# Up-projections of two FFNs as seven block products, with hidden tiles through DRAM and stacked low-rank products

## The chip, the cores and the metric

The kernel runs on one core of a Trainium2 chip. The core has TensorE (PE in the profile, with its weight loads as PEld), VectorE (DVE), ScalarE (ACT), GpSimd (POOL) and SyncE (SP, which here issues most DMAs). The metric is the device time of one execution in microseconds; the number given for a kernel is the median of its runs.

## The reference

Two transformer blocks follow each other on 1024 tokens of 1024 features, in float32. In short:

```
# block 1
h = x + concat(pool_mixer, ssm_mixer) @ w_out
u = rmsnorm(h, norm_ffn)
h = h + (silu(u @ w_gate) * (u @ w_up)) @ w_down          # D_FF = 2816
x = rmsnorm(h, norm_final)
# block 2
z = rmsnorm(x, g_mix) @ w_in      # latents of MLA, r, k, v and low-rank inputs of RWKV, gates
w = w0 + tanh(w_lo) @ w2;  a = sigmoid(a0 + a_lo @ a2);  g = sigmoid(g_lo) @ g2   # ranks 64, 64, 128
x = x + (gate_a * mla(z) + gate_b * rwkv7(z)) @ w_out
u = rmsnorm(x, g_ffn)
x = x + square(relu(u @ w_ffn_up)) @ w_ffn_down           # D_FF_2 = 4096
x = rmsnorm(x + sigmoid(rmsnorm(x, g_ple) @ w_ple_gate) * (p @ w_ple_proj), g_final)
```

## The kernel before

Each float32 operand of a product is split into a high part (rounded to the matmul's type, a cast on ScalarE, L103 or L122) and a low part (the rest, a subtraction on VectorE, L104 or L124); `mm3` (L137) makes hi·hi, hi·lo and lo·hi, three matmuls of a 128x128 weight block with 512 columns each, accumulated in PSUM. `weights` (L127) loads 128x1024 raw weights into one of two buffers "wr" and splits them, into two buffers each of "wh" and "wl", or, kept longer, into slots "wk". `slot` hands out 128x1024 tiles of a common pool.

A *unit* (`unit_t`) is one tile of 128 outputs for all 1024 tokens: 2 halves of the tokens x 8 blocks of the input x 3 = 48 matmuls into a PSUM tile "big" of 128x1024, of which there are four (two in the RWKV stage). `norm_units` makes the first two units: transposes of the scaled tokens for one half, split into "hn" (L195 on ScalarE, L197 on VectorE), then the units' matmuls on it, then the other half.

`ffn` walks over the hidden tiles, 22 in FFN1 (gate and up for each) and 32 in FFN2, in chunks of three. Each hidden tile is activated (L667 and L668, or L674 and L675) and split, its w_down rows are loaded and split, and `tok_matmul` (L242) multiplies the chunk by w_down for 8 token tiles x 2 halves, which VectorE adds to the residual `res` in SBUF (L659).

`rwkv_z` (L924) makes the token-shifted r, k and v by units (`project`), and in `low_rank(0)` and `(1)` products with w2 and a2, on operands of 64 rows, 2 x 4 output tiles x 2 halves x 3 = 48 matmuls; each output goes through one of two buffers "zo" to DRAM (zr).

The program is written in this order, and a scheduler orders each engine's queue by priority of program order and by when it reckons things to be ready; the engines then run their queues in order, with semaphores between them.

## Time and profile before

| | |
|---|---|
| median of 3 runs | 2983.57 us (2983.23 to 2987.06) |
| profiled execution | 2986.8 us, span 2985.0 us, mean granted TensorE clock 0.98 |
| TensorE | busy 2885.8 us, 14937 matmuls recorded |
| VectorE, ScalarE, GpSimd | 1301.5, 842.9 and 159.6 us |
| DMA | 227.46 MB |

A busy engine at 97% with a chain that lies mostly on it says which engine sets the time; where it waits is seen from windows of the stages and from the timeline.

### The profile page before, as it was taken

Reading aid. Unit: us, or ns where it says so; the run is one execution under the profiler, and the core shown is the slowest. Engines: PE = TensorE matmul, PEld = TensorE weight load, DVE = VectorE, ACT = ScalarE, POOL = GpSimd, SP = SyncE. Lnnn points to the kernel's source line nnn. Section 1 sums busy time; section 2 is a strip of 40 time slices with the busy share of each in tenths; the row PEclk is TensorE's granted clock in tenths of the full one; section 3 lists DMA queues with packets and bytes.
Section 4 is the critical chain, followed back from the end, with each engine's and each line's share of the span. In section 5 each row is a group of like instructions: output and inputs, shape, how many; then the busy total and the mean of one; then the engine's idle time right before and its main releaser. Section 6 shows DMA issues by size and latency. Waiting matters only on the chain.

```text
span 2985.0 us, 36005 instructions
## 1 busy us (share of the span) xinstructions
PE 2885.8 (97%) x14937; PEld 2299.3 (77%) x14937; DVE 1301.5 (44%) x1980; ACT 842.9 (28%) x1275; POOL 159.6 (5%) x343
## 2 busy tenths in 40 slices
...
GB/s 135 103 120 161 36 36 50 64 39 33 57 64 33 74 155 127 116 132 75 108 60 117 117 53 24 40 119 162 43 36 43 56 50 51 56 43 43 43 78 99
DMA packets 136115, 227.46 MB, mean 76 GB/s; under 512 B 60880, under 2 KB 82000, under 8 KB 135952
## 3 DMA queue, kind: packets, MB, share of 16 engines
...
## 4 chain that ended last, share of the span: by engine, by line
PE 85%; DVE 5%; POOL 3%; DMA 3%; ACT 2%; issue 2%; SPq 0%; ACTq 0%; DVEq 0%; POOLq 0%
PE big L139 25%; PE big L140 24%; PE big L141 24%; PE big L833 2%; POOL wt L1165 1%; POOL tt L1166 1%; PE ps L861 1%; PE ps L1137 1%; PE chain L855 1%; PE chain L854 1%; DVE t L836 0%; PE chain L139 0%; PE chain L140 0%; PE chain L141 0%; PE big L192 0%
## 5 line engine op out<-in xcount | busy, mean ns | idle before, releaser
L139 PE MATMUL big<-hn,wh 128*128 128x512 f32 x1872 | 747.2, 400 | 7.2 <-DVE zo L937 4.0
L140 PE MATMUL big<-hn,wh 128*128 128x512 f32 x1872 | 746.4, 399 | 1.9 <-DVE hn L197 1.9
L141 PE MATMUL big<-hn,wl 128*128 128x512 f32 x1872 | 744.0, 398 | 0.0
L139 PEld LDWEIGHTS big<-hn,wh 128*128 128x128 f32 x1872 | 353.2, 189 | 93.3 <-issue 5.9
L140 PEld LDWEIGHTS big<-hn,wh 128*128 128x128 f32 x1872 | 353.9, 189 | 86.5 <-DVE hn L197 3.2
L141 PEld LDWEIGHTS big<-hn,wl 128*128 128x128 f32 x1872 | 354.6, 189 | 85.0 <-DVE wl L104 2.5
L103 ACT CAST wh<-wr 128x1024 fp32r<-128x1024 f32 (+1 forms) x142 | 141.8, 999 | 935.0 <-PE big L140 742.0
L104 DVE TENSOR_TENSOR wl<-wr,wh 128x1024 fp32r<-128x1024 f32 (+1 forms) x142 | 166.1, 1170 | 425.7 <-ACT wh L103 424.9
L141 PE MATMUL big<-wk,a 128*128 128x512 f32 x864 | 338.4, 394 | 0.0
L140 PE MATMUL big<-wk,a 128*128 128x512 f32 x864 | 337.9, 393 | 0.1
L139 PE MATMUL big<-wk,a 128*128 128x512 f32 x864 | 334.7, 395 | 1.8 <-ACT wk L103 1.8
L659 DVE TENSOR_TENSOR r<-big,r 128x1024 f32<-128x1024 f32 x144 | 176.2, 1224 | 314.4 <-PE big L141 314.2
L139 PEld LDWEIGHTS big<-wk,a 128*128 128x128 f32 x864 | 160.9, 188 | 43.5 <-ACT wk L103 7.6
L140 PEld LDWEIGHTS big<-wk,a 128*128 128x128 f32 x864 | 162.2, 188 | 38.7 <-DVE wk L104 0.8
L141 PEld LDWEIGHTS big<-wk,a 128*128 128x128 f32 x864 | 162.2, 188 | 37.4
L674 ACT ACTIVATE zo<-big 128x1024 f32<-128x1024 f32 x32 | 32.9, 1027 | 368.3 <-PE big L141 368.3
L668 DVE TENSOR_TENSOR zo<-zo,big 128x1024 f32<-128x1024 f32 x22 | 26.9, 1221 | 205.7 <-PE big L141 205.7
L104 DVE TENSOR_TENSOR wk<-wr,wk 128x1024 fp32r<-128x1024 f32 (+1 forms) x86 | 100.3, 1173 | 31.6 <-ACT wk L103 31.5
L139 PE MATMUL big<-wk,mx 128*128 128x512 f32 x256 | 100.8, 400 | 2.6 <-ACT wk L103 2.6
L140 PE MATMUL big<-wk,mx 128*128 128x512 f32 x256 | 101.9, 398 | 1.0 <-DVE wk L104 1.0
L141 PE MATMUL big<-wk,mx 128*128 128x512 f32 x256 | 101.1, 395 | 0.0
L103 ACT CAST wk<-wr 128x1024 fp32r<-128x1024 f32 (+1 forms) x86 | 85.2, 1001 | 44.2 <-DMA wr<-in_w_out_dram 36.0
(408 smaller groups left out, 3639.4 us busy)
## 6 DMA issues: line engine op xcount, KB each, us to landing
wr<-in_w_ffn_up_dram SPq DMA_DIRECT2D x32, 512.0 KB, 3.2
wr<-in_w_ffn_down_dram SPq DMA_DIRECT2D x32, 512.0 KB, 3.2
zr<-zo SPq DMA_DIRECT2D x24, 512.0 KB, 3.5
wr<-in_w_gate_dram SPq DMA_DIRECT2D x22, 512.0 KB, 3.2
wr<-in_w_up_dram SPq DMA_DIRECT2D x22, 512.0 KB, 3.3
wr<-in_w_down_dram SPq DMA_DIRECT2D x22, 512.0 KB, 3.2
wr<-in_w_gates_dram SPq DMA_DIRECT2D x16, 512.0 KB, 4.6
gd<-zo SPq DMA_DIRECT2D x16, 512.0 KB, 3.1
```

Source lines behind the costliest of these rows:

```text
L103: nc.scalar.copy(hi, x)
L104: nc.vector.tensor_tensor(lo, x, hi.bitcast(F32), ALU.subtract)
L139: nc.tensor.matmul(ps, lhsT=w[0], rhs=x[0], start=start, stop=False)
L140: nc.tensor.matmul(ps, lhsT=w[0], rhs=x[1], start=False, stop=False)
L141: nc.tensor.matmul(ps, lhsT=w[1], rhs=x[0], start=False, stop=stop)
L659: nc.vector.tensor_tensor(res[t], ps, res[t], ALU.add)
L674: nc.scalar.activation(s, ps, AF.Relu)
L833: nc.tensor.matmul(sc[:, c:c + m], lhsT=q[:, i * P:(i + 1) * P], rhs=k[:, c:c + m], start=True, stop=c + m < n, skip_group_check=True)
L854: nc.tensor.matmul(acc[:, c0:H], lhsT=w, rhs=hi, start=t == 0, stop=False, skip_group_check=True)
L855: nc.tensor.matmul(acc[:, c0:H], lhsT=w, rhs=lo, start=False, stop=t == last, skip_group_check=True)
L861: nc.tensor.transpose(pt[:, j * P:(j + 1) * P], ps[j][:, t * P:(t + 1) * P], self.ident)
L1137: nc.tensor.matmul(ps[:, pt * P:(pt + 1) * P], lhsT=bk[c2][rows, c, pt, :, :], rhs=ar[c2][rows, c, pt, :, :], start=True, stop=True)
```

## The change

`ffn` stores `res` to DRAM (rd) at its start and reads it back before the down-projections. The input and two neighbouring hidden tiles are taken as 2 x 2 blocks, and a pair's up-projection is made with seven products of 4 input blocks x 3 = 12 matmuls instead of eight: `pair_weights` makes the sums S1 to S4 of weight blocks on GpSimd and splits them, `pair_products` accumulates the products in four PSUM tiles of 128x512 and puts the outputs together with copies on ScalarE and additions on VectorE and one on GpSimd. The sums T1 to T4 of input blocks are made by `sums` on GpSimd, while the first hidden tiles (two with gate and up in FFN1, four in FFN2) are made by units as before. `norm_blocks` makes plain float32 copies of the normed input ("bf") as well, for these sums, with the low part of the first four blocks on GpSimd. All hidden tiles are stored in DRAM (hd), read back and split in the down phase, whose chunks start with one tile (FFN1) or two (FFN2).

In `rwkv_z` the operands of low_rank(0) and (1) are stacked as high and low part in 128 rows, so two matmuls make what three made (32 in place of 48), and the outputs go to slot "z" instead of "zo", those of `project` too.

Lines taken out stand in the kernel above; of the diff's new lines these matter:

```diff
...
+    def mm3(self, ps, w, x, start, stop, **kw):
+        nc = self.nc
+        nc.tensor.matmul(ps, lhsT=w[0], rhs=x[0], start=start, stop=False, **kw)
+        nc.tensor.matmul(ps, lhsT=w[0], rhs=x[1], start=False, stop=False, **kw)
+        nc.tensor.matmul(ps, lhsT=w[1], rhs=x[0], start=False, stop=stop, **kw)
...
+    def norm_blocks(self, res, g, groups=(3, 1)):
+        nc = self.nc
+        hn = [[None, None] for _ in range(NK)]
+        x = {n: [None] * 4 for n in ("B11", "B21", "B22", "T1", "T2", "T3", "T4")}
+        plain = [[None] * 4 for _ in range(2)]
+        def norm_half(half):
+            xs, t = [], 4 * half
+            for n in groups:
+                xs += self.scaled(res[t:t + n])
+                t += n
+            for k in range(4):
+                ps = self.big()
+                for j in range(2):
+                    for i in range(4):
+                        c = (4 * j + i) * P
+                        nc.tensor.transpose(ps[:, c:c + P], xs[i][:, (k + 4 * j) * P:(k + 4 * j + 1) * P], self.ident)
+                p1, p2 = self.halves(ps)
+                g1, g2 = self.col(g, k), self.col(g, k + 4)
+                f1, f2 = self.halves(self.slot("bf"))
+                plain[half][k] = f1, f2
+                h1, l1 = hn[k][half] = self.half_pair("hn")
+                h2, l2 = hn[k + 4][half] = self.half_pair("hn")
+                nc.scalar.activation(h1, p1, AF.Identity, scale=g1)
+                nc.vector.tensor_scalar(f1, p1, g1, None, ALU.mult)
+                nc.scalar.activation(h2, p2, AF.Identity, scale=g2)
+                nc.vector.scalar_tensor_tensor(l2, p2, g2, h2.bitcast(F32), ALU.mult, ALU.subtract)
+                nc.scalar.activation(f2, p2, AF.Identity, scale=g2)
+                nc.gpsimd.tensor_tensor(l1, f1, h1.bitcast(F32), ALU.subtract)
+                if half == 0:
+                    x["B11"][k], x["B21"][k] = hn[k][0], hn[k + 4][0]
+                else:
+                    x["B22"][k] = hn[k + 4][1]
+        def sums(k):
+            (b11, b21), (b12, b22) = plain[0][k], plain[1][k]
+            t12, t34 = self.slot("tf"), self.slot("tf")
+            t1, t2, t3, t4 = *self.halves(t12), *self.halves(t34)
+            nc.gpsimd.tensor_tensor(t1, b12, b11, ALU.subtract)
+            nc.gpsimd.tensor_tensor(t2, b22, t1, ALU.subtract)
+            nc.gpsimd.tensor_tensor(t3, b22, b12, ALU.subtract)
+            nc.gpsimd.tensor_tensor(t4, b21, t2, ALU.subtract)
+            for t, names in ((t12, ("T1", "T2")), (t34, ("T3", "T4"))):
+                hi, lo = self.slot("hn", F32R), self.slot("hn", F32R)
+                self.split(t, hi, lo)
+                for n, h, l in zip(names, self.halves(hi), self.halves(lo)):
+                    x[n][k] = h, l
+        return hn, norm_half, x, sums
+    def pair_weights(self, src):
+        nc = self.nc
+        raw = [self.wp.tile([P, 1024], F32, tag="wr", name=self.nm("wr"), bufs=2) for _ in range(2)]
+        for r, s in zip(raw, src):
+            nc.sync.dma_start(r, s)
+        a11, a12, a21, a22 = *self.halves(raw[0]), *self.halves(raw[1])
+        w = {}
+        def put(x, *names):
+            hi, lo = self.slot("wc", F32R), self.slot("wc", F32R)
+            self.split(x, hi, lo)
+            for n, h, l in zip(names, self.halves(hi), self.halves(lo)):
+                w[n] = h, l
+        put(raw[0], "A11", "A12")
+        yield w
+        s12, s34 = (self.wp.tile([P, 1024], F32, tag=t, name=self.nm("ws"), bufs=2) for t in ("wh", "wl"))
+        s1, s2, s3, s4 = *self.halves(s12), *self.halves(s34)
+        nc.gpsimd.tensor_tensor(s1, a21, a22, ALU.add)
+        nc.gpsimd.tensor_tensor(s2, s1, a11, ALU.subtract)
+        put(s12, "S1", "S2")
+        nc.gpsimd.tensor_tensor(s3, a11, a21, ALU.subtract)
+        nc.gpsimd.tensor_tensor(s4, a12, s2, ALU.subtract)
+        put(s34, "S3", "S4")
+        w["A22"] = self.half_pair("wc")
+        self.split(a22, *w["A22"])
+        yield w
+    def pair_products(self, weights, x, c1, c2):
+        nc = self.nc
+        def product(ps, a, b, start):
+            for k in range(4):
+                self.mm3(ps, tuple(v[:, k * P:(k + 1) * P] for v in w[a]), x[b][k], start and k == 0, k == 3, skip_group_check=True)
+        w = next(weights)
+        pa, pb = (self.big()[:, 0:H] for _ in range(2))
+        p1, p5 = self.halves(self.slot("pr"))
+        product(pa, "A11", "B11", True)
+        nc.scalar.copy(p1, pa)
+        product(pb, "A12", "B21", True)
+        nc.vector.tensor_tensor(c1[:, 0:H], pb, p1, ALU.add)
+        next(weights)
+        pc, pd = (self.big()[:, 0:H] for _ in range(2))
+        u2, u3 = self.halves(self.slot("pr"))
+        product(pc, "S1", "T1", True)
+        nc.scalar.copy(p5, pc)
+        product(pa, "S2", "T2", False)
+        nc.scalar.copy(u2, pa)
+        product(pd, "S3", "T3", True)
+        nc.vector.tensor_tensor(u3, pd, u2, ALU.add)
+        product(pc, "S4", "B22", False)
+        nc.vector.tensor_tensor(c1[:, H:2 * H], pc, u2, ALU.add)
+        nc.gpsimd.tensor_tensor(c2[:, H:2 * H], u3, p5, ALU.add)
+        product(pd, "A22", "T4", False)
+        nc.vector.tensor_tensor(c2[:, 0:H], pd, u2, ALU.add)
+    def ffn(self, res, g, nf, chunks, up, act, w_down, last=lambda: None):
+        nc = self.nc
+        rd = self.dp.tile([T, D], F32, name=self.nm("rd"))
+        hd = self.dp.tile([nf, P, T], F32, name=self.nm("hd"))
+        for t in range(8):
+            nc.sync.dma_start(rd[t * P:(t + 1) * P, :], res[t])
+        hn, norm_half, x, sums = self.norm_blocks(res, g)
         nu = len(up)
+        n0 = 4 // nu
+        units = [(u, j) for j in range(n0) for u in up]
+        made = self.norm_units(norm_half, hn, [self.weights(u[j]) for u, j in units[0:2]])
+        made = list(made)
+        for k in range(4):
+            sums(k)
+        for j in range(n0):
+            while len(made) < nu:
+                u, i = units[4 - nu * (n0 - j) + len(made)]
+                made.append(self.unit_t(self.weights(u[i]), hn))
+            h = self.zo()
+            act(h, *made[:nu])
+            made = made[nu:]
+            nc.sync.dma_start(hd[j], h)
+        def hidden(f):
+            h = self.weights(hd[f], keep=True)
+            wd = self.weights(w_down[f * P:(f + 1) * P, :], keep=True)
+            return [tuple(v[:, half * H:half * H + H] for v in h) for half in range(2)], wd
+        ready = []
+        for j in range(n0, nf, 2):
+            outs = []
+            for i, u in enumerate(up):
+                if j == nf - 2 and i == nu - 1:
+                    ready.append(hidden(0))
+                c = [self.zo() if i == 0 else self.slot("cu") for _ in range(2)]
+                outs.append(c)
+                self.pair_products(self.pair_weights((u[j], u[j + 1])), x, *c)
+            if j == nf - 2:
+                res = self.load_res(rd)
+            for i in range(2):
+                act(outs[0][i], *(c[i] for c in outs))
+                nc.sync.dma_start(hd[j + i], outs[0][i])
+        f = 0
         for nch in chunks:
             acts, wd = [], []
             for _ in range(nch):
+                h, w = ready.pop() if ready else hidden(f)
+                acts.append(h)
+                wd.append(w)
                 f += 1
             def evac(t, ps):
                 nc.vector.tensor_tensor(res[t], ps, res[t], ALU.add)
+                if t == 3 and f == nf:
                     last()
             self.tok_matmul(acts, wd, evac)
+        return res
+    def swiglu(self, out, g, u):
+        nc = self.nc
+        nc.scalar.activation(out, g, AF.Silu)
+        nc.vector.tensor_tensor(out, out, u, ALU.mult)
+    def relu2(self, out, h):
+        nc = self.nc
+        nc.scalar.activation(out, h, AF.Relu)
+        nc.vector.tensor_tensor(out, out, out, ALU.mult)
...
-        self.ffn(res, "norm_ffn", (3, 3, 3, 3, 3, 3, 4), (a["w_gate"], a["w_up"]), self.swiglu, a["w_down"], self.ple_inputs)
+        res = self.ffn(res, "norm_ffn", FF1, (1,) + (3,) * 7, (a["w_gate"], a["w_up"]), self.swiglu, a["w_down"], self.ple_inputs)
...
-        lora = []
+        stacked, wide = [], None
         for u in range(2):
             z = self.slot("z")
             shift(u, first[u], z)
             if u == 0:
                 nc.scalar.activation(z[0:64], z[0:64], AF.Tanh)
+                for hi, lo in ((slice(0, 64), slice(64, 128)), (slice(64, 128), slice(0, 64))):
+                    x = self.slot("lo", F32R)
+                    nc.scalar.copy(x[hi], z[hi])
+                    nc.vector.tensor_tensor(x[lo], z[hi], x[hi].bitcast(F32), ALU.subtract)
+                    stacked.append(x)
             else:
                 nc.scalar.activation(z, z, AF.Sigmoid)
-            lora.append(self.split_halves(z, "lo"))
+                wide = self.split_halves(z, "lo")
         self.rope_keys(hn, w_kpe)
-        wl = self.weights(a["w_lora"], keep=True)
+        wl = self.weights(a["w_lora"][:, H:2 * H], keep=True, n=H)
+        raw = self.wp.tile([P, 1024], F32, tag="wr", name=self.nm("wr"), bufs=2)
+        for i in range(2):
+            for h in range(2):
+                nc.sync.dma_start(raw[h * 64:h * 64 + 64, i * H:i * H + H], a["w_lora"][i * 64:i * 64 + 64, 0:H])
+        ws = tuple(self.slot("wk", F32R) for _ in range(2))
+        self.split(raw, *ws)
         def low_rank(i):
-            x, rows, c0 = ((0, slice(0, 64), 0), (0, slice(64, 128), 0), (1, slice(0, 128), 512))[i]
...
-                c = c0 + pt * P
                 for half in range(2):
                     sl = slice(half * H, half * H + H)
-                    self.mm3(ps[:, sl], tuple(w[rows, c:c + P] for w in wl), tuple(v[rows] for v in lora[x][half]), True, True)
-                z = self.zo()
+                    if i < 2:
+                        c = i * H + pt * P
+                        for j, w in enumerate(ws):
+                            nc.tensor.matmul(ps[:, sl], lhsT=w[:, c:c + P], rhs=stacked[i][:, sl], start=j == 0, stop=j == 1)
+                    else:
+                        self.mm3(ps[:, sl], tuple(w[:, pt * P:pt * P + P] for w in wl), wide[half], True, True)
+                z = self.slot("z")
...
         def project(u0):
             for u in range(u0, u0 + 4):
-                z = self.zo()
+                z = self.slot("z")
...
-        self.ffn(res, "g_ffn_2", (3,) * 10 + (2,), (a["w_ffn_up"],), self.relu2, a["w_ffn_down"])
+        res = self.ffn(res, "g_ffn_2", FF2, (2,) + (3,) * 10, (a["w_ffn_up"],), self.relu2, a["w_ffn_down"])
...
```

The first place is an up pair of FFN1. On VectorE, before, each up unit has one split of weights (wl) around the multiplication L668:

```order
L104 TENSOR_TENSOR wl_3418<-wr_3415,wh_3417 128x1024
L668 TENSOR_TENSOR zo_3400<-zo_3400,big_3351 128x1024
L104 TENSOR_TENSOR wl_3473<-wr_3470,wh_3472 128x1024
L124 SCALAR_TENSOR_TENSOR a_3403<-zo_3400,a_3403 128x512
L124 SCALAR_TENSOR_TENSOR a_3404<-zo_3400,a_3404 128x512
```

Now, from the end of a pair of w_gate (zo) into one of w_up (cu); ws are S1,S2 and S3,S4, wc their low parts, pr the copies of products:

```order
L104 TENSOR_TENSOR wc_3248<-ws_3243,wc_3247 128x1024
L104 TENSOR_TENSOR wc_3254<-ws_3244,wc_3253 128x1024
L738 TENSOR_TENSOR zo_3204<-big_3215,pr_3216 128x512
L104 TENSOR_TENSOR wc_3257<-wr_3207,wc_3257 128x512
L104 TENSOR_TENSOR wc_3336<-wr_3331,wc_3335 128x1024
L747 TENSOR_TENSOR pr_3262<-big_3261,pr_3262 128x512
L749 TENSOR_TENSOR zo_3204<-big_3260,pr_3262 128x512
L752 TENSOR_TENSOR zo_3205<-big_3261,pr_3262 128x512
L738 TENSOR_TENSOR cu_3329<-big_3340,pr_3341 128x512
L104 TENSOR_TENSOR wc_3373<-ws_3368,wc_3372 128x1024
L104 TENSOR_TENSOR wc_3379<-ws_3369,wc_3378 128x1024
```

The addition L738 stands behind the two subtractions in the w_gate pair and ahead of them in the w_up pair. TensorE there goes from the second product (wc_3335, wc_3336) to S1·T1, S2·T2 and S3·T3 (high parts wc_3372 and wc_3378, low part wc_3373):

```order
L141 MATMUL big_3340<-hn_2544,wc_3336 128x512
L139 MATMUL big_3385<-hn_2780,wc_3372 128x512
L140 MATMUL big_3385<-hn_2781,wc_3372 128x512
L139 MATMUL big_3339<-hn_2780,wc_3372 128x512
L140 MATMUL big_3339<-hn_2781,wc_3372 128x512
L139 MATMUL big_3386<-hn_2784,wc_3378 128x512
L141 MATMUL big_3385<-hn_2780,wc_3373 128x512
```

Five matmuls on high parts stand ahead of the first on a low part.

The second place is VectorE at the start of FFN1's down phase (r_914 to r_921 are the token tiles of res, wk splits of hidden tiles and w_down rows, two for each hidden tile):

```order
L808 TENSOR_TENSOR r_918_5518<-big_5568,r_918_5518 128x1024
L104 TENSOR_TENSOR wk_5603<-wr_5600,wk_5602 128x1024
L808 TENSOR_TENSOR r_919_5519<-big_5576,r_919_5519 128x1024
L808 TENSOR_TENSOR r_920_5520<-big_5584,r_920_5520 128x1024
L808 TENSOR_TENSOR r_921_5521<-big_5592,r_921_5521 128x1024
L104 TENSOR_TENSOR wk_5609<-wr_5606,wk_5608 128x1024
```

Before, the splits of a chunk's last hidden tile and w_down rows stood ahead of the eight evacuations; now the two splits of hidden tile 1 stand among and behind those of the chunk of tile 0.

The third place is ScalarE in a pair of FFN2. Before, around one hidden tile:

```order
L103 CAST wh_16617<-wr_16615 128x1024
L674 ACTIVATE zo_16600<-big_16551 128x1024
L122 ACTIVATE a_16603<-zo_16600 128x512
L122 ACTIVATE a_16604<-zo_16600 128x512
L103 CAST wk_16611<-wr_16609 128x1024
```

Now, one pair (A11,A12 of the next pair are wc_16839; the activations L821 are those of the pair before; L736, L743 and L745 copy products out of PSUM):

```order
L103 CAST wc_16839<-wr_16835 128x1024
L821 ACTIVATE zo_16702<-zo_16702 128x1024
L821 ACTIVATE zo_16703<-zo_16703 128x1024
L736 COPY pr_16845<-big_16843 128x512
L103 CAST wc_16876<-ws_16872 128x1024
L103 CAST wc_16882<-ws_16873 128x1024
L103 CAST wc_16886<-wr_16836 128x512
L743 COPY pr_16845<-big_16889 128x512
L745 COPY pr_16891<-big_16843 128x512
```

The second activation, of the output that GpSimd adds up, stands ahead of the copy of the next pair's first product and of the casts of S1,S2 and S3,S4.

## Rows read from the trace of the kernel before

**Rows 1.** The page: busy time by engine, and shares of the chain that ended last.

```profile
PE 2885.8 (97%) x14937; PEld 2299.3 (77%) x14937; DVE 1301.5 (44%) x1980; ACT 842.9 (28%) x1275; POOL 159.6 (5%) x343
...
PE 85%; DVE 5%; POOL 3%; DMA 3%; ACT 2%; issue 2%; SPq 0%; ACTq 0%; DVEq 0%; POOLq 0%
```

**Rows 2.** Windows of the two FFN stretches (window, length, then each engine's busy time and records).

```profile
330.00:1060.00 730.00, 729.99 (x3162) 590.26 (x3161) 219.10 (x241) 135.97 (x173) 0.00 (x0) 1.00 0.15 52
2175.00:2850.00 675.00, 675.00 (x2905) 543.68 (x2904) 251.65 (x237) 128.53 (x156) 0.00 (x0) 1.00 0.14 46
```

**Rows 3.** The page's groups of lines: products of norm output and weights.

```profile
L139 PE MATMUL big<-hn,wh 128*128 128x512 f32 x1872 | 747.2, 400 | 7.2 <-DVE zo L937 4.0
```

**Rows 4.** Timeline of TensorE in FFN1 (start, duration).

```profile
620.05 0.39 PE L139 MATMUL big<-hn,wh 128*128 128x512 f32 x1
620.28 0.39 PE L140 MATMUL big<-hn,wh 128*128 128x512 f32 x1
```

**Rows 5.** Windows of low_rank(0) and (1) and of what follows.

```profile
1172.10:1193.90 21.80, 19.28 (x49) 13.70 (x48) 2.91 (x3) 11.49 (x11) 0.00 (x0) 0.58 0.56 216
1193.90:1199.40 5.50, 5.50 (x14) 4.31 (x14) 2.18 (x6) 4.31 (x5) 0.00 (x0) 0.51 0.61 198
```

**Rows 6.** Timeline of ScalarE there.

```profile
1175.58 1.28 ACT L960 ACT_TABLE_LOAD   x1 [1.52 <-DVE zo L937]
...
1189.90 2.33 ACT L960 ACTIVATE zo<-big,vec 128x1024 f32<-128x1024 f32 x2 [3.42 <-DMA zr<-zo]
```

**Rows 7.** Windows of two stalls: before rwkv_z's units, and at FFN2's end.

```profile
1132.80:1137.00 4.20, 0.24 (x2) 0.00 (x0) 3.02 (x3) 4.13 (x4) 0.00 (x0) 1.00 0.20 56
1137.00:1141.40 4.40, 4.32 (x12) 3.44 (x13) 2.98 (x4) 2.34 (x3) 0.00 (x0) 0.61 0.76 304
2850.00:2862.00 12.00, 10.17 (x44) 7.62 (x43) 6.11 (x6) 5.11 (x6) 0.00 (x0) 1.00 0.44 155
```

**Rows 8.** Groups of ScalarE by form (count, busy us, mean ns).

```profile
L103 ACT CAST wh<-wr 128x1024 fp32r<-128x1024 f32 x130 | 136.1, 1048 | 914.5 <-PE big L140 732.8 <-DMA wr<-in_w_ffn_up_dram 140.1 <-issue 26.6
...
L195 ACT ACTIVATE hn<-big,vec 128x512 fp32r<-128x512 f32 x64 | 38.7, 697 | 81.3 <-PE big L192 81.0
...
L674 ACT ACTIVATE zo<-big 128x1024 f32<-128x1024 f32 x32 | 32.9, 1027 | 368.3 <-PE big L141 368.3
L864 ACT CAST pts<-ps 128x512 fp32r<-128x512 f32 x48 | 27.3, 587 | 15.3 <-PE ps L861 15.2
...
L103 ACT CAST wk<-wr 128x512 fp32r<-128x512 f32 x8 | 4.7, 619 | 9.2 <-DMA wr<-in_w_out_dram 7.7 <-DMA usd<-zo 1.5
```

**Rows 9.** Groups of VectorE by form.

```profile
L104 DVE TENSOR_TENSOR wl<-wr,wh 128x1024 fp32r<-128x1024 f32 x130 | 159.4, 1226 | 416.4 <-ACT wh L103 415.7
...
L197 DVE SCALAR_TENSOR_TENSOR hn<-big,vec,hn 128x512 fp32r<-128x512 f32 x64 | 43.4, 745 | 18.7 <-ACT hn L195 15.6 <-PE big L192 3.0
...
L1363 DVE TENSOR_TENSOR r<-r,zo 128x512 f32<-128x512 f32 x16 | 11.1, 691 | 0.5
```

**Rows 10.** GpSimd: its widest addition (group by form), and a timeline in rwkv.

```profile
L877 POOL TENSOR_TENSOR o<-os 64x512 f32<-64x512 f32 x16 | 20.4, 1272 | 183.8 <-DVE os L876 114.5 <-DMA os<-rsd 65.3 <-DVE t L845 4.1
...
1623.31 0.44 POOL L1166 TENSOR_TENSOR tt<-tt,wt 128x133 f32<-128x133 f32 x1
1623.84 1.48 POOL L1165 TENSOR_TENSOR wt<-d,tt 128x126 f32<-128x126 f32 x1
```

**Rows 11.** DMA issues (KB each, median us to landing).

```profile
wr<-in_w_ffn_up_dram SPq DMA_DIRECT2D x32, 512.0 KB, 3.2
...
zr<-zo SPq DMA_DIRECT2D x24, 512.0 KB, 3.5
...
r<-r SPq DMA_DIRECT2D x8, 512.0 KB, 8.0
```

**Rows 12.** Timeline of VectorE beside those of GpSimd.

```profile
1622.41 1.50 DVE L1248 TENSOR_TENSOR tt<-tt,ps 128x512 f32<-128x512 f32 x2 [2.51 <-PE ps L1044]
1623.83 1.22 DVE L104 TENSOR_TENSOR wl<-wr,wh 128x1024 fp32r<-128x1024 f32 x1
```

26 lines of the change are left out of this document (removed).

## The prediction

> **What bounds the kernel now.** I read the page first: TensorE is busy for 97% of the span, and the chain of work that ended last lies on it for 85% [rows 1]. Then the windows of the two FFN stretches, where the change works: 730 us with 3162 matmuls recorded and 0.01 us idle, 675 us with 2905 and no idle at all, both at granted clock 1.00, the higher of its two levels, 2.4 GHz [rows 2]. So there time is matmuls times the step between them. The group of lines agrees: the 1872 matmuls of L139 on hn and wh waited 7.2 us in the whole program [rows 3]. The step is the distance of two starts in the timeline, 620.28 - 620.05 = 0.23 us (0.2315 over a longer run of rows; 675.00/2905 = 0.232) [rows 2, 4], not the 0.39 us of one record, since they overlap. ScalarE, VectorE and above all GpSimd (159.6 us) have time to spare [rows 1].
>
> **Term 1, the matmuls taken out.** FFN1 before: 22 hidden tiles x 2 projections x 48 matmuls = 2112. After: 2 tiles plain (192) and 10 pairs x 2 projections x 7 products x 12 = 1680, so 240 fewer. FFN2: 32 x 48 = 1536 before; 4 plain (192) and 14 pairs x 84 = 1176 after, 168 fewer. The down-projections stay. 408 x 0.2315 = **94.5 us** less. A product is 12 x 0.2315 = 2.78 us, a pair 19.45.
>
> **Term 2, the low-rank products.** The 48 matmuls of low_rank(0) and (1) stand in 21.8 us at mean clock 0.58, and the next 14 rows take 5.5 us at 0.51, that is near the 1.2 GHz level [rows 5]: 27.3 us. ScalarE waits there for stores of the two zo buffers (3.42 us at one place), and TensorE, two PSUM tiles deep, for ScalarE [rows 6]. After: 32 matmuls, outputs in slot "z", no store in the way. TensorE needs 4 x 0.2315 = 0.93 us a tile, ScalarE 1.17 (2.33 for two), so 8 x 1.17 plus a table load of 1.28 = 10.6 [rows 6], and the 14 at the full clock 3.2: 14 us. Gain **13**. Should the clock drop again, the 46 at the rate of the slow stretch, 5.50/14 = 0.39, take 18: gain 9.
>
> **Term 3, small stalls removed.** At the end of FFN2 the last chunk's activation and splits leave TensorE 10.17 us busy of 12 [rows 7]; after, hidden tiles are long made: **-3** (0 to -4).
>
> **Term 4, FFN starts, +8.** A PSUM tile of transposes had four readers (ScalarE 0.70 twice, VectorE 0.75 twice [rows 8, 9]); now there are five, three of them on ScalarE: 2.1 us instead of 1.4, 8 times per FFN, 5.6 us at most by that row, and a bit more where the two engines alternate. I take 4 for each FFN (1.5 to 7).
>
> **Term 5, the plain tiles that follow, +10.** sums() puts 16 GpSimd operations of 128x512 ahead. The row for their price is the add of 64x512, 1272 ns; one of 128x133 takes 0.44 us [rows 10]; by the first, with as many columns, I take 1.3 (0.44 x 512/133 = 1.7 if time went by the column alone). ScalarE's casts of T12 and T34 wait for them, and the casts of the third and fourth unit's weights are queued behind. Sums take 16 x 1.3 = 21 us after the second half's transposes, while two units keep TensorE for 22: the casts come some us late. I take 6 in FFN1 and 4 in FFN2 (0 to 14 together).
>
> **Term 6, FFN1's up pairs, +6.5.** The order of VectorE puts the add of the second product (L738) ahead of the low part of S1,S2 there. The product ends at 5.56, the add at 5.56 + 0.69 = 6.25, the subtraction at 7.48 [rows 9]. TensorE has five matmuls on high parts in front, so it wants the low part at 5.56 + 5 x 0.2315 = 6.72: 0.7 us, 10 times, less some slack. In gate pairs and in FFN2 the splits stand first, and the low part is there at about 5.7 to 5.9, no wait above 0.3.
>
> **Term 7, from up to down, +12.** In FFN1 only hidden tile 0 is ready; its chunk is 48 matmuls, 11.1 us. The splits of tile 1 and its w_down stand on VectorE behind the evacuations r_918 and r_921, so the second is done 2.4 us after the chunk's end. There are two raw buffers, and a load lands 3.2 us after its issue [rows 11]; the four splits still missing follow at +3.7, +8, +9 and +12.3 for the last high part (cast 1.05, subtraction 1.23 [rows 8, 9]). TensorE can do 6 matmuls of the first output tile meanwhile: about 10 us idle. FFN2's first chunk is 22.2 us long, and 2 remain.
>
> **Term 8, clock, +4.** After a stretch with TensorE busy 0.24 of 4.2 us the granted clock was 0.61 in the next 4.4 us, which then held 12 matmuls in place of 19 [rows 7]: about 1.7 us for a stall of that length. Terms 4, 5 and 7 make two or three such.
>
> **Term 9, everything else in a pair, +5**: 34 pairs x 0.15 us for semaphores and half-bank PSUM tiles that wait for one copy (0 to 35, that is up to 1 us a pair). What hides a pair's other work: ScalarE per pair 3 x 1.05 + 0.6 + 3 x 0.59 = 5.5 us and one activation or two [rows 8], VectorE 3 x 1.23 + 5 x 0.69 = 7.1 and one or two multiplications [rows 9], both well under 19.45. SyncE's two loads a pair and the new stores of hidden tiles (3.5 us a store [rows 11]) go through queues that moved 46 to 52 GB/s there [rows 2]; res goes out and back in 8 us [rows 11], behind the last pair. In the down phase each hidden tile adds a load, a cast and a subtraction where split_halves made the same before; a chunk has 33 us for six of each.
>
> Sum: -94.5 - 13 - 3 + 8 + 10 + 6.5 + 12 + 4 + 5 = **-65 us**. The profiled execution took 2986.8 us, 1.8 over its span and 3.2 over the median of the runs, 2983.57; a change inside the program leaves both, so 2986.8 - 65 = 2921.8 for a profile, and **2919** for the median.
>
> **GpSimd, the rule that speaks against it.** In a pair GpSimd makes S1 to S4 and one output sum. The second raw tile of the next pair can be loaded when the low part of A22 is made (8.3) and is there at 11.6; 5 x 1.3 brings the sum to 18.1, relu to 20.2 (it also waits for the seventh product), the copy of the first product follows, and S12's cast ends by 23.5, wanted at 19.45 + 5.56 = 25.0. So GpSimd may take 2.15 us per operation before ScalarE's order makes TensorE wait. The trace has what makes it longer: the add of 128x126 at 1623.84 took 1.48 us while VectorE ran an operation with both operands in SBUF (L104, 1.22 us from 1623.83); the one before it, 128x133 in 0.44, lay beside VectorE operations that read PSUM [rows 10, 12]. The Trainium skill, GPSIMD Engine Reference, Elementwise — side-by-side cycle accounting, says to keep elementwise work on VectorE, GpSimd needing about twice its time; an estimate by its figure (4497 ns for 2048 columns) is 1.1 us for 512, and the sum would not change. The Trainium skill, SBUF — State Buffer, section SBUF: two separate sides, calls the port that both engines share an exclusive lock held for an instruction; the row of 1.48 agrees, and taken to the letter it gives the waits of the next sentence, or rival (c) if every operation meets one. Two such VectorE operations stand in GpSimd's stretch of a pair, 2 x 1.23 = 2.5 us: 18.1 becomes 20.6, still under 22.35, where it would begin to cost.
>
> **Rivals.**
> (a) GpSimd late: at 1.7 us an operation and three VectorE operations met (3.7 us) the sum ends at 11.6 + 8.5 + 3.7 = 23.8, 1.4 us after 22.35, at 14 + 10 ends of pairs: 34 us, or 50 with the sums of term 5 late as well: 2953 to 2969. For it: the contention rows. Against: 1272 ns for 512 columns.
> (b) The weights late: each pair's two loads wait for two raw buffers, and a store ahead of them on SyncE waits for the activation. A load held up to 14 instead of 8.3 moves GpSimd's chain past 22.35 by 1.5 to 2 us: 34 x 2 = 68, and the time is that of before, within 0.2%. Against: the landing of 3.2 us [rows 11] leaves 5 us.
> (c) Slower than before: the ring from one pair's weights to the next one's is longer than a pair. It is the load 3.2, five GpSimd operations, relu 1.03, the copy 0.59, the casts 1.05, 1.05 and 0.62, and A22's subtraction 0.69: 8.2 us + 5 operations, against 19.45. It decides at (19.45 + 65/34 - 8.2)/5 = 2.6 us an operation; if each took 1.7 and met VectorE for 1.0 more (1.48 against 0.44 above), TensorE would wait 8.2 + 13.5 - 19.45 = 2.25 us 34 times: 77 - 65 = +12, 2996. For it: VectorE is busy in a third of a pair with both operands in SBUF. Against: only some operations meet one.
> (d) The matmuls go but the step grows, because weights and operands change at every product: at 0.24 us instead of 0.2315 the roughly 5800 matmuls of both FFNs cost 49 us more, 2968. Against it: before, too, each matmul has its own weight load, and there is no idle between them [rows 2, 3].
>
> **The numbers.** Forecast (terms as above, 2891 to 2947) 0.73; (a) and (d) 0.15; (b) 0.04; (c) 0.06; 0.02 that the added terms are nearly all absent (-100, 2884). A measurement of this kernel tells a change of about 0.2% (6 us) from none. Faster by more than that: 0.90; within it: 0.04; slower: 0.06. Range: low end 2890 (terms 4 to 9 at about half), high end 2960 (the forecast with (a) in its lower half).
>
> **What the next profile would show.** Windows of the FFNs with TensorE's count down by 240 and 168 and its step unchanged (term 1; a step over 0.235 is (d)). A stall of 8 to 12 us after the first chunk of FFN1's down phase, ended by a split (term 7). 0.5 to 1 us before the low part of S1,S2 in each up pair and none in gate pairs (term 6). GpSimd's 128x512 operations at 1.3 us, some at 2.5 (else (a)). ScalarE's eight sigmoids of low_rank 1.1 to 1.2 us apart, with clock 1.00 (term 2). I am wrong if TensorE sits idle at every pair's start or at its third product, or if the clock falls inside the pairs.

## The result and the profile after

The changed kernel takes 2949.43 us (median of 3 runs, 2948.05 to 2949.82) against 2983.57: 34.1 us less, a ratio of 0.9881 with a 95% interval of 0.9867 to 0.9894. The forecast was 2919, so the way and the range were right and the gain is about half of what the sum gave. In the profiled executions the span falls from 2985.0 to 2946.2, by 38.8; that execution of before was the slowest of its three, so 65 is to be held against 38.8.

The page of the changed kernel, busy times and the groups of its matmuls (the last two fields: idle time just before the group, and what ended most of it):

```profile
PE 2792.1 (95%) x14513; PEld 2216.2 (75%) x14513; DVE 1527.1 (52%) x2155; ACT 977.0 (33%) x1424; POOL 497.7 (17%) x561
...
L141 PE MATMUL big<-hn,wc 128*128 128x512 f32 x952 | 374.9, 395 | 8.7 <-DVE wc L104 8.7
L139 PE MATMUL big<-hn,wc 128*128 128x512 f32 x952 | 374.8, 394 | 1.3 <-ACT wc L103 1.3
L140 PE MATMUL big<-hn,wc 128*128 128x512 f32 x952 | 375.0, 394 | 0.0
L139 PE MATMUL big<-hn,wh 128*128 128x512 f32 x816 | 331.5, 409 | 29.6 <-ACT wh L103 25.9
L139 PE MATMUL big<-wk,wk 128*128 128x512 f32 x864 | 339.5, 395 | 4.9 <-ACT wk L103 4.1
...
L140 PE MATMUL big<-hn,wh 128*128 128x512 f32 x816 | 331.4, 406 | 6.9 <-POOL hn L676 6.1
L141 PE MATMUL big<-hn,wl 128*128 128x512 f32 x816 | 330.6, 406 | 4.1 <-DVE wl L104 4.1
```

TensorE is busy 93.7 us less than in [rows 1], and the span lost only 38.8, so 54.9 us of idle time are new. The group hn,wc is the seven products: 2856 matmuls that waited 10 us in all. The idle time lies on hn,wh, the plain units, which waited for the cast of their weights, and to a smaller part for GpSimd's low part of hn (L676). The chain of waits on this page accounts for 27% of the span only, so I went by windows, at places that the timeline showed (window, length, busy time and records of PE, PEld, DVE, ACT and POOL, granted clock, DMA share, GB/s):

```profile
300.00:380.00 80.00, 67.81 (x306) 52.56 (x305) 43.60 (x57) 34.19 (x46) 46.08 (x28) 0.96 0.12 46
380.00:780.00 400.00, 391.91 (x1681) 314.71 (x1680) 177.42 (x181) 126.61 (x163) 142.94 (x96) 1.00 0.25 88
785.00:815.00 30.00, 25.64 (x98) 18.57 (x97) 20.81 (x20) 8.38 (x8) 0.00 (x0) 0.94 0.45 152
1098.30:1116.30 18.00, 0.13 (x1) 0.00 (x0) 14.72 (x16) 4.80 (x5) 0.00 (x0) 0.63 0.24 78
1116.30:1121.30 5.00, 4.93 (x13) 3.52 (x14) 1.52 (x2) 1.05 (x1) 0.00 (x0) 0.62 0.87 243
1165.00:1177.00 12.00, 10.37 (x34) 6.82 (x35) 1.44 (x3) 10.16 (x9) 0.00 (x0) 0.86 0.90 349
2140.00:2190.00 50.00, 39.20 (x163) 29.17 (x164) 33.87 (x49) 27.00 (x40) 32.06 (x21) 0.93 0.10 35
2190.00:2460.00 270.00, 269.99 (x1167) 218.80 (x1166) 145.94 (x139) 102.07 (x125) 109.03 (x71) 1.00 0.30 107
2460.00:2490.00 30.00, 26.41 (x104) 20.18 (x103) 13.75 (x13) 8.37 (x10) 5.69 (x4) 0.94 0.74 274
```

In order: FFN1's start (12.2 us idle), its pairs (8.1), its way into the down phase (4.4), the place in rwkv_z and the 5 us behind it, the sigmoids of the low-rank stretch, FFN2's start (10.8), its pairs (0.01), its last pair and its way down (3.6). In the pairs the step is 269.99/1167 = 0.231 us, as in [rows 2]. The place in rwkv_z is the surprise: 18 us without matmuls, where before 4.2 were lost [rows 7]. Read from its timeline (start, duration, engine, line; in brackets how long the engine sat idle before, and for whom):

```profile
1106.11 1.15 ACT L882 ACTIVATE ang<-ang,cst 128x1024 f32<-128x1024 f32 x1 [12.33 <-DVE ang L881]
...
1108.56 1.55 ACT L103 CAST wk<-wr 128x512 fp32r<-128x512 f32 x2
...
1111.19 0.69 DVE L104 TENSOR_TENSOR wk<-wr,wk 128x512 fp32r<-128x512 f32 x1
1111.91 0.33 SPq L129 DMA_DIRECT2D wr<-in_w_rwkv_dram  x1
...
1115.24 1.04 ACT L103 CAST wh<-wr 128x1024 fp32r<-128x1024 f32 x1 [5.13 <-DMA wr<-in_w_rwkv_dram]
...
1116.33 0.80 PE L139 MATMUL big<-hn,wh 128*128 128x512 f32 x1 [17.90 <-ACT wh L103]
```

Read it from the bottom. TensorE waits for weights of project(6), which are cast as soon as they land; their load is issued only when a raw buffer is free, after the subtraction at 1111.19; that is a split of w_lora, whose cast stands on ScalarE behind the rotary tables' sine (L882), and the sine waited 12.3 us for VectorE. The change loads w_lora into two raw buffers where one load took one, and there are only two. In the kernel before, the order on ScalarE was the other one: project's weights and a shift stood ahead of the sine.

```profile
1132.84 1.04 ACT L103 CAST wh<-wr 128x1024 fp32r<-128x1024 f32 x1 [16.32 <-PE big L140]
1133.79 1.11 ACT L936 ACTIVATE zo<-big,vec 128x1024 f32<-128x1024 f32 x1
...
1136.21 2.19 ACT L736 ACTIVATE ang<-ang,cst 128x1024 f32<-128x1024 f32 x2
```

So the 4.2 us of [rows 7] were not a wait for the sine; TensorE waited there for the shift on VectorE (L937, [rows 3]).

The low-rank stretch itself did nearly what was forecast: its eight sigmoids, first and last start,

```profile
L1121 ACT ACTIVATE z<-big,vec x8: 1113/1115/1117, 1166.2 to 1175.8; 128x1024 f32<-128x1024 f32 x8
```

lie within 9.6 us, where the old ones took 21.4, and the granted clock around them was 0.86 (the forecast had 1.00) instead of 0.58 and 0.51 [rows 5]. The 21.4 us are not all waits for stores: before, a piece of the WKV preparation (L1066) stood on ScalarE ahead of the eighth sigmoid, and in the changed kernel it comes later.

```profile
1193.45 1.28 ACT L1066 ACT_TABLE_LOAD   x1 [1.22 <-DMA sg<-zr]
1195.88 1.06 ACT L1066 ACTIVATE P<-sg 128x1024 f32<-128x1024 f32 x1 [1.15 <-DVE sg L1063]
1196.96 1.28 ACT L960 ACT_TABLE_LOAD   x1
1198.25 1.11 ACT L960 ACTIVATE zo<-big,vec 128x1024 f32<-128x1024 f32 x1
```

For the stages I took five starts in each trace: the first addition to res ahead of FFN1 (in before 274.4), the first shift of RWKV (1106.0), the first and last maximum of the attention's softmax (1766.1, 1957.1) and the last addition ahead of FFN2 (2153.6). Their differences, and the rest to the span's end, in us:

| profiled kernel | FFN1 and on to RWKV | RWKV to attention | of it: to the first low-rank sigmoid | first to last of these eight | attention | to FFN2 | FFN2 to the end | span |
|---|---|---|---|---|---|---|---|---|
| before | 831.6 | 660.1 | 70.9 | 21.4 | 191.0 | 196.5 | 831.4 | 2985.0 |
| changed | 808.0 | 668.9 | 84.4 | 9.6 | 189.4 | 196.4 | 809.7 | 2946.2 |
| e1_ffn_only | 808.9 | 656.7 | 70.8 | 20.8 | 191.9 | 195.1 | 808.8 | 2935.6 |
| e2_lora_slot | 809.1 | 659.1 | 74.4 | 9.8 | 192.1 | 196.7 | 811.2 | 2944.9 |
| e3_sums_late | 806.4 | 668.4 | 85.1 | 8.7 | 192.0 | 197.9 | 809.8 | 2950.6 |
| e4_add_late | 798.6 | 669.7 | 85.7 | 9.6 | 192.1 | 197.1 | 811.0 | 2941.9 |
| e5_changed_again | 810.9 | 668.6 | 84.4 | 9.5 | 203.9 | 197.9 | 806.6 | 2962.4 |
| e6_sums_on_dve | 803.5 | 667.0 | 84.3 | 9.6 | 197.0 | 197.4 | 802.2 | 2940.1 |
| e7_lora_slot_zo | 811.4 | 661.3 | 70.8 | 20.5 | 200.4 | 198.0 | 806.5 | 2951.6 |
| e8_lora_slot_zo_project | 811.9 | 650.9 | 70.5 | 9.8 | 197.9 | 197.4 | 808.1 | 2939.0 |
| e9_combined | 794.5 | 653.8 | 70.6 | 9.8 | 190.9 | 197.2 | 800.6 | 2911.3 |
| e10_combined_low_on_dve | 789.9 | 651.4 | 70.3 | 9.7 | 192.0 | 195.7 | 801.3 | 2905.5 |
| e11_pair_sums_on_dve | 811.0 | 666.3 | 84.3 | 9.7 | 192.4 | 195.3 | 806.3 | 2945.9 |
| e12_before_again | 831.6 | 658.6 | 72.2 | 21.0 | 203.6 | 197.4 | 831.6 | 2995.5 |

So the change gave 23.6 us up to RWKV and 21.7 from FFN2 on, and took 8.8 between RWKV's first unit and the attention, where 13 were to be gained.

### The profile page after: what moved, and what is told of

Same layout as the page of the kernel before. It is cut to its first block, busy times and chain, and to the rows that moved or that the text cites. A ratio compares the mean times of both kernels' runs of the same rounds, so it can differ in the third digit from the quotient of the medians.

```text
span 2946.2 us, 36439 instructions
## 1 busy us (share of the span) xinstructions
PE 2792.1 (95%) x14513; PEld 2216.2 (75%) x14513; DVE 1527.1 (52%) x2155; ACT 977.0 (33%) x1424; POOL 497.7 (17%) x561
## 5 line engine op out<-in xcount | busy, mean ns | idle before, releaser
L141 PE MATMUL big<-hn,wc 128*128 128x512 f32 x952 | 374.9, 395 | 8.7 <-DVE wc L104 8.7
L139 PE MATMUL big<-hn,wc 128*128 128x512 f32 x952 | 374.8, 394 | 1.3 <-ACT wc L103 1.3
L140 PE MATMUL big<-hn,wc 128*128 128x512 f32 x952 | 375.0, 394 | 0.0
L139 PE MATMUL big<-hn,wh 128*128 128x512 f32 x816 | 331.5, 409 | 29.6 <-ACT wh L103 25.9
L139 PE MATMUL big<-wk,wk 128*128 128x512 f32 x864 | 339.5, 395 | 4.9 <-ACT wk L103 4.1
L140 PE MATMUL big<-wk,wk 128*128 128x512 f32 x864 | 342.3, 396 | 1.2 <-DVE zo L1081 0.6
L141 PE MATMUL big<-wk,wk 128*128 128x512 f32 x864 | 342.3, 396 | 0.0
L140 PE MATMUL big<-hn,wh 128*128 128x512 f32 x816 | 331.4, 406 | 6.9 <-POOL hn L676 6.1
L141 PE MATMUL big<-hn,wl 128*128 128x512 f32 x816 | 330.6, 406 | 4.1 <-DVE wl L104 4.1
L103 ACT CAST wk<-wr 128x1024 fp32r<-128x1024 f32 (+1 forms) x139 | 139.6, 1022 | 428.7 <-PE big L140 196.4
L141 PEld LDWEIGHTS big<-hn,wc 128*128 128x128 f32 x952 | 178.8, 188 | 55.6 <-DVE wc L104 14.1
L104 DVE TENSOR_TENSOR wk<-wr,wk 128x1024 fp32r<-128x1024 f32 (+1 forms) x139 | 164.1, 1187 | 99.6 <-ACT wk L103 99.3
L139 PEld LDWEIGHTS big<-hn,wc 128*128 128x128 f32 x952 | 179.0, 188 | 42.4 <-ACT wc L103 2.0
L140 PEld LDWEIGHTS big<-hn,wc 128*128 128x128 f32 x952 | 179.0, 188 | 41.6
L139 PEld LDWEIGHTS big<-hn,wh 128*128 128x128 f32 x816 | 155.7, 191 | 71.8 <-ACT wh L103 28.7
L139 PEld LDWEIGHTS big<-wk,wk 128*128 128x128 f32 x864 | 162.5, 188 | 45.4 <-ACT wk L103 6.2
L140 PEld LDWEIGHTS big<-wk,wk 128*128 128x128 f32 x864 | 163.4, 189 | 41.0 <-DVE wk L104 1.9
L140 PEld LDWEIGHTS big<-hn,wh 128*128 128x128 f32 x816 | 156.4, 192 | 48.1 <-POOL hn L676 10.2
L141 PEld LDWEIGHTS big<-wk,wk 128*128 128x128 f32 x864 | 163.3, 189 | 37.5
L104 DVE TENSOR_TENSOR wl<-wr,wh 128x1024 fp32r<-128x1024 f32 (+2 forms) x76 | 89.3, 1175 | 192.4 <-ACT wh L103 190.0
L141 PEld LDWEIGHTS big<-hn,wl 128*128 128x128 f32 x816 | 156.3, 192 | 42.1 <-DVE wl L104 6.0
```

Of the source, the lines that this page charges most:

```text
L103: nc.scalar.copy(hi, x)
L104: nc.vector.tensor_tensor(lo, x, hi.bitcast(F32), ALU.subtract)
L139: nc.tensor.matmul(ps, lhsT=w[0], rhs=x[0], start=start, stop=False, **kw)
L140: nc.tensor.matmul(ps, lhsT=w[0], rhs=x[1], start=False, stop=False, **kw)
L141: nc.tensor.matmul(ps, lhsT=w[1], rhs=x[0], start=False, stop=stop, **kw)
```

## The experiments

Three sets of four kernels, each set on one chip with its own runs of the kernel before. Ratios are to those; what the table shows by stage is the finer measure, since the attention, which no edit touches, took 189 to 204 us. Each row of the table is one execution; the FFN stages of kernels with the same FFN code differ by up to 5 us in it.

**Which part costs, and which gains.** e1_ffn_only puts the old `rwkv_z` back into the changed kernel:

```diff
-        stacked, wide = [], None
+        lora = []
...
-        wl = self.weights(a["w_lora"][:, H:2 * H], keep=True, n=H)
-        raw = self.wp.tile([P, 1024], F32, tag="wr", name=self.nm("wr"), bufs=2)
+        wl = self.weights(a["w_lora"], keep=True)
...
-                z = self.slot("z")
+                z = self.zo()
```

> The changed kernel with rwkv_z as it was before (low-rank products of 48 matmuls, zo buffers, one load of w_lora). Theory A (the changed low-rank loads take both raw weight buffers, so that project(6) waits behind the sine activations): the 18 us idle before project(6) is gone and the old 4 us stall and the old 27 us low-rank stretch are back; net about -4 us against the changed kernel, 2945 to 2946. Rival B (the idle comes from the FFN part, which delivers its slots or buffers later): the idle of some 18 us stays, and with the old low-rank stretch the time is 10 to 14 us above the changed kernel, about 2961.

Measured: 2939.68 us, ratio 0.9827 (0.9813 to 0.9841). The first two stages of `rwkv_z` are back at 70.8 and 20.8, those of before; TensorE's wait at that place is 4.06 us again, for VectorE as before. Rival B, the FFN's slots, falls. The change of `rwkv_z` as it stands costs: 668.9 against 656.7 us between the same two marks, 12.2 where A expected about 4.

**The raw buffer.** e2_lora_slot gives the second load of w_lora a tile of the pool:

```diff
-        raw = self.wp.tile([P, 1024], F32, tag="wr", name=self.nm("wr"), bufs=2)
+        raw = self.slot("wr")
```

> The changed kernel, but the four 64-row pieces of w_lora are loaded into a pool slot instead of a second raw weight buffer. Theory A: one raw buffer stays free for project(6), TensorE no longer idles 18 us there, and the low-rank stretch keeps its gain: 15 to 19 us less than the changed kernel, about 2932. Rival B: no change, 2949.

Measured: 2946.52 us, ratio 0.9839 (0.9825 to 0.9854). The stage shrinks from 84.4 to 74.4, and the low-rank stretch keeps its 9.8. A holds, with 10 us instead of 15 to 19: TensorE still waits 8.0 us, now for the PSUM tile that the rotary keys are read from. In e8 below, where project's outputs go to zo, that wait is 4.05 and the stage 70.5.

**The queue behind GpSimd's sums.** e3_sums_late:

```diff
         made = list(made)
-        for k in range(4):
-            sums(k)
         for j in range(n0):
...
             nc.sync.dma_start(hd[j], h)
+        for k in range(4):
+            sums(k)
```

> The changed kernel with the sums T1 to T4 written behind the first plain hidden tiles, so that ScalarE casts the weights of the third and fourth unit ahead of most casts of T. Theory A (ScalarE's queue order behind GpSimd's sums makes the wait of 6.7 us in FFN1 and 5.4 us in FFN2): FFN1's wait falls by 3 to 4 us, as the weights now wait for the first two casts of T and the Silu only; FFN2's order hardly changes, 0 to 1 us. Total 3 to 5 us less, about 2945. Rival B (the weights are late by themselves, their raw loads or the wh buffers): no change; and if the sums then come too late, TensorE waits before the first S1*T1 and it is 3 or more us slower.

Measured: 2949.60 us, ratio 0.9857 (0.9841 to 0.9873), which does not show a gain of this size. In FFN1's timeline, changed kernel first, then e3 (the two starts of plain units that wait for weights):

```profile
353.78 0.79 PE L139 MATMUL big<-hn,wh 128*128 128x512 f32 x1 [6.02 <-ACT wh L103]
355.67 0.79 PE L139 MATMUL big<-hn,wh 128*128 128x512 f32 x1 [0.68 <-ACT wh L103]
```

```profile
352.73 0.50 PE L139 MATMUL big<-hn,wh 128*128 128x512 f32 x1 [2.69 <-ACT wh L103]
353.68 0.50 PE L139 MATMUL big<-hn,wh 128*128 128x512 f32 x1 [0.21 <-ACT wh L103]
355.14 0.79 PE L141 MATMUL big<-hn,wl 128*128 128x512 f32 x1 [0.55 <-DVE wl L104]
```

6.7 us become 3.45, as A expected of FFN1, whose stage is 1.6 us shorter, and FFN2's stage is unchanged. What remains still waits for the first two casts of T, so the order is only part of it.

**The sums off GpSimd.** e6_sums_on_dve:

```diff
-            nc.gpsimd.tensor_tensor(t1, b12, b11, ALU.subtract)
+            nc.vector.tensor_tensor(t1, b12, b11, ALU.subtract)
```

and so for t2, t3 and t4.

> The changed kernel with the sums T1 to T4 of input blocks on VectorE instead of GpSimd. Theory A (ScalarE's casts stand behind sums that take GpSimd 1.3 us each, 2.3 beside VectorE): 16 x 0.69 us on VectorE, the casts of T and of the weights come several us earlier, the wait of 6.7 us in FFN1 falls to about 2 and FFN2's 5.4 to 1 to 3, together 6 to 9 us less and about 2 less of slow clock. Rival B (five reads of each PSUM tile and the norm's chain are what makes the starts long, not the sums): the waits before the third unit's weights stay within 2 us of what they were; total 0 to 2 us.

Measured: 2946.37 us, ratio 0.9844 (0.9825 to 0.9862); the changed kernel beside it, e5_changed_again, 2959.13 and 0.9889 (0.9872 to 0.9905).

> The changed kernel unaltered, as the base for the three beside it: 0.988 of the time before, within the interval of the first measurement. It also says whether the stretch from the last projection of RWKV to the second FFN (870.7 us in the changed kernel's trace, 867.4 before, 863.7 with the old rwkv_z) differs by more than it scatters: under both theories below it should be 870 to 874 again.

The same 20 us of FFN1's start, changed kernel (first trace) and e6:

```profile
340.00:360.00 20.00, 12.53 (x43) 9.10 (x43) 12.70 (x8) 9.53 (x11) 19.77 (x13) 0.83 0.15 52
```

```profile
340.00:360.00 20.00, 18.83 (x81) 14.97 (x81) 18.78 (x23) 11.86 (x14) 1.85 (x2) 1.00 0.22 79
```

TensorE is busy 18.83 of 20 us instead of 12.53, with the clock at 1.00 instead of 0.83. GpSimd was busy throughout there, and with it ScalarE's queue stood; changed kernel, then the cast of the same weights in e6:

```profile
343.38 1.28 POOL L687 TENSOR_TENSOR tf<-bf,tf 128x512 f32<-128x512 f32 x1
...
345.78 3.57 DVE L104 TENSOR_TENSOR hn<-tf,hn 128x1024 fp32r<-128x1024 f32 x2 [4.70 <-ACT hn L103]
346.00 2.27 POOL L686 TENSOR_TENSOR tf<-bf,bf 128x512 f32<-128x512 f32 x1
...
351.73 1.04 ACT L103 CAST hn<-tf 128x1024 fp32r<-128x1024 f32 x1 [2.27 <-POOL tf L687]
352.68 1.04 ACT L103 CAST wh<-wr 128x1024 fp32r<-128x1024 f32 x1
```

```profile
345.40 1.05 ACT L103 CAST wh<-wr 128x1024 fp32r<-128x1024 f32 x1 [0.47 <-PE big L140]
```

TensorE's waits for these weights, 6.7 us in FFN1 and 5.4 in FFN2, are gone in e6. FFN1 gains 7.4 us and FFN2 4.4 against e5: theory A, with a little more than the 8 to 11 us expected. e5's own expectation failed: its stretch behind the last projection came out 15.8 us longer than in the first trace, of which 14.5 are attention, the part that scatters in the unchanged kernel too (e12).

**The order in up pairs.** e4_add_late:

```diff
-        nc.vector.tensor_tensor(c1[:, 0:H], pb, p1, ALU.add)
         next(weights)
+        nc.vector.tensor_tensor(c1[:, 0:H], pb, p1, ALU.add)
```

> The changed kernel with the addition of the second product (into c1) written behind the weight sums, so that VectorE makes the low parts of S1,S2 first in FFN1's up pairs too. Theory A (this order is the cause of the idle 0.8 us in each up pair): 0.8 us less in 10 pairs, 8 us, about 2941, and L141 big<-hn,wc idles near 0. Rival B (the low part is late because S1,S2 themselves are late from GpSimd): idle time only moves to another matmul, 0 to 2 us.

Measured: 2943.44 us, ratio 0.9837 (0.9824 to 0.9851). The wait in a pair of the changed kernel, and the group in e4:

```profile
406.17 0.50 PE L141 MATMUL big<-hn,wc 128*128 128x512 f32 x1 [0.82 <-DVE wc L104]
```

```profile
L141 PE MATMUL big<-hn,wc 128*128 128x512 f32 x952 | 375.4, 394 | 0.9 <-DVE wc L104 0.9
```

8.7 us of idle time become 0.9, and FFN1 is 9.4 us shorter than in the first trace, where 8 were expected. A holds.

**The slots named z.** e7_lora_slot_zo takes e2 and sends all outputs of `project` and `low_rank` through zo again; e8_lora_slot_zo_project leaves those of low_rank(0) and (1) in slots:

```diff
-                z = self.slot("z")
+                z = self.slot("z") if i < 2 else self.zo()
...
-                z = self.slot("z")
+                z = self.zo()
                 shift(u, self.unit_t(self.weights(a["w_rwkv"][u]), hn), z)
```

> The changed kernel with the 64-row pieces of w_lora in a pool slot (as in the run e2_lora_slot) and all outputs of project and low_rank through the two zo buffers as before, the 32 stacked matmuls kept. Theory A (slots named z fill the pool of 38, so that the first load of the WKV preparation is issued 84 us later than before and TensorE later waits for that preparation): that load goes out in the middle of low_rank again, the 7.5 us wait about 100 us after the last projection is gone, that stretch falls from 870 to about 864 to 867; but ScalarE waits for stores again in low_rank, 18 to 21 us for its eight outputs instead of 9.6. Rival B (the later wait comes from something else): the stretch stays 870 to 874. Time by A: 5 to 9 us less than the changed kernel.

> As e7_lora_slot_zo, but the eight outputs of low_rank(0) and (1) still go to slots z; only project and low_rank(2) use zo. Theory A: both gains, eight outputs in 9.6 us and the stretch behind the last projection 864 to 867: 16 to 20 us less than the changed kernel. Rival B: the stretch stays 870 to 874, and the gain is that of e2_lora_slot alone, some 10 us.

Measured: e7 2953.37 us, ratio 0.9866 (0.9849 to 0.9882); e8 2940.78, 0.9816 (0.9798 to 0.9834). The load of the first WKV input goes out early again in e7; changed kernel, then e7:

```profile
1273.83 0.69 SPq L1211 DMA_DIRECT2D sg<-zr  x1
```

```profile
1167.97 0.38 SPq L1211 DMA_DIRECT2D sg<-zr  x1
```

So the slots do push it back, by 106 us in these traces. But theory A of its cost holds only in part: e7's wait for the WKV matrices is 5.4 us where the changed kernel has 7.5, and from the last of the eight sigmoids to the attention the table gives 570.0 in e7 and 570.6 in e8 (its column to the attention minus the two parts of it beside), against 574.9 in the changed kernel and 567.8 before. By these alone some 4 of 7 us come back. All traces of the table say less: 572.3 to 574.9 with project's outputs in slots (seven traces, mean 574.1), 570.0 to 573.4 with them in zo (e7 to e10, mean 571.4), 565.1 to 567.8 with the old `rwkv_z` (three, mean 566.1), so some 3 of 8 us. What the rest is was not settled. The low-rank part answers as expected: 20.5 us through zo, 9.8 through slots, and from its first sigmoid to the attention e8 has 580.4 us and e7 590.5. e8 is the best `rwkv_z`, 650.9 us to the attention, 9.2 under before and 18.0 under the changed kernel; with the same `rwkv_z` e9 and e10 below have 653.8 and 651.4.

**The contention.** In the changed kernel two of GpSimd's four sums (the other two, L718 and L719, take 1439 and 1547 ns) and VectorE's subtraction for A11,A12 by form (count, busy, mean ns):

```profile
L716 POOL TENSOR_TENSOR ws<-ws,wr 128x512 f32<-128x512 f32 x34 | 65.7, 1932 | 0.0
...
L715 POOL TENSOR_TENSOR ws<-wr 128x512 f32<-128x512 f32 x34 | 46.6, 1372 | 370.3 <-DMA wr<-in_w_ffn_up_dram 143.1 <-DMA wr<-in_w_gate_dram 120.3 <-DMA wr<-in_w_up_dram 106.8
```

```profile
L104 DVE TENSOR_TENSOR wc<-wr,wc 128x1024 fp32r<-128x1024 f32 x34 | 67.2, 1977 | 102.5 <-ACT wc L103 102.5
```

The subtraction takes 1.98 us where [rows 9] gave 1.23. e11_pair_sums_on_dve:

```diff
-        nc.gpsimd.tensor_tensor(s1, a21, a22, ALU.add)
+        nc.vector.tensor_tensor(s1, a21, a22, ALU.add)
```

and so for s2 to s4 and the output sum.

> The changed kernel with S1 to S4 and the output sum of each pair on VectorE, GpSimd keeps the sums T and the norm's low part. Theory A (GpSimd and VectorE lengthen one another's operations, to 1.9 and 2.0 us, but this never reaches TensorE inside a pair): VectorE's subtraction for A11,A12 falls from 1.98 to 1.23 us, and TensorE's idle time in the pairs stays as it is, within 3 us of the changed kernel. Rival B (the contention costs time): 0.3 to 1 us less in each of 34 pairs, 10 to 30 us less.

Measured: 2948.87 us, ratio 0.9855 (0.9837 to 0.9872). In e11:

```profile
L104 DVE TENSOR_TENSOR wc<-wr,wc 128x1024 fp32r<-128x1024 f32 x34 | 41.5, 1219 | 2.5 <-ACT wc L103 2.5
```

The subtraction is back at 1.22, and the products still wait 8.8 us in all, FFN1 is at 811.0 and FFN2 at 806.3, as in e5. A: inside the pairs the contention is real, and no cost of it to TensorE can be seen.

**Together.** e9_combined has the edits of e4, e6 and e8; e10_combined_low_on_dve has also

```diff
-                nc.gpsimd.tensor_tensor(l1, f1, h1.bitcast(F32), ALU.subtract)
+                nc.vector.tensor_tensor(l1, f1, h1.bitcast(F32), ALU.subtract)
```

> The changed kernel with the edits of e4_add_late, e6_sums_on_dve and e8_lora_slot_zo_project together. Theory A (three separate causes: the order in up pairs, ScalarE's queue behind GpSimd's sums, both raw buffers held by w_lora): their gains add up, from the stage tables 9.4 + 11.7 + 13.9 + about 4 = 39 us less than the changed kernel, 0.975 to 0.978 of the time before. Rival B (they hide one another, since a stall removed is taken up by the next): less than 28 us, above 0.980.

> e9_combined with the low part of the norm's first four blocks on VectorE too (from the plain copy), so that GpSimd has no part in the norm. Theory A: TensorE's waits for GpSimd's hn (6 us in both FFNs) shrink by VectorE's 0.69 against 1.28 us: 2 to 4 us less than e9_combined. Rival B: VectorE's own queue is the limit of the norm (four operations of 0.7 per PSUM tile instead of three), so it is the same or 1 to 3 us slower.

Measured: e9 2912.12 us, ratio 0.9730 (0.9713 to 0.9747); e10 2909.84 and 0.9726 (0.9707 to 0.9744). By the spans e9 has 34.9 us less than the changed kernel's first trace, where A expected 39 and B less than 28; the ratio is a little better than A's 0.975 to 0.978. The causes add up, nearly, and the gain over the kernel before is 2.7%, more than twice that of the changed kernel. e10's step cannot be told from none by the time; by the stages FFN1 has 4.6 us less, about what that stage scatters, and FFN2 0.7 more. What A named did shrink: TensorE's wait on L140 for the low part of hn is 3.8 us in e10 and 7.7 in e9.

**The kernel before, again.**

> The kernel before on the chip of these runs, for its stages: if the attention stretch scatters with the chip and not with the change, it takes 191 to 204 us here as in the runs beside it, where the kernels don't differ; the stretch from the first RWKV unit to the attention should be 660 us again.

One execution: 2997.27 us. Its attention takes 203.6 us, its way from RWKV to the attention 658.6, both FFN stages are those of the first trace within 0.2. The attention scatters without the change; the three kernels beside it here had 191 to 192, so it is not the chip alone. The trace shows where the time goes:

```profile
1839.16 1.25 POOL L877 TENSOR_TENSOR o<-os 64x512 f32<-64x512 f32 x1 [16.83 <-DMA os<-rsd]
1840.44 0.97 ACT L864 CAST pts<-ps 128x512 fp32r<-128x512 f32 x2 [2.81 <-POOL o L877]
...
1841.08 0.64 PE L854 MATMUL chain<-pts,v 128*128 128x512 f32 x1 [2.57 <-ACT pts L864]
```

GpSimd waited for a load (os, read from DRAM), ScalarE's cast of pts for GpSimd, and TensorE for the cast, 7.3 us in all in this attention; the mean granted clock of the attention was 0.96, and 0.98 in the first trace of the kernel before. In the five traces with an attention of 197 us and more, ScalarE waited 3.4 to 8.0 us in all for this addition (L877, in the changed kernels L1023); in the nine with 189 to 192, 1.0 at most. Why the load lands late in some executions stays open.

## Why the prediction was half right

The time lies in the stated range, but above the 2947 that the terms were given, in the part that was put there for rival (a). Rival (a) did not happen; that the miss of term 2 fell inside its part is luck.

- **Term 1** held: 424 matmuls fewer were recorded, its 408 and the 16 of the low-rank products, with the step at 0.231; TensorE's busy time fell by 93.7 us; rival (d) falls.
- **Term 2 is the step that failed.** It said of the change in `rwkv_z` 'no store in the way' and a gain of 13, and counted the eight sigmoids only (21.4 to 9.6: 11.8 us, right). It gave the five loads of w_lora no price. They take both raw buffers, so the weights of project(6) come to stand behind the split of w_lora, and with it behind the sine's 12.3 us wait for VectorE, where before they stood ahead of the sine; so 13.5 us are lost ahead of the stretch (70.9 to 84.4) and 7.1 behind it. With e1, e2 and e8 this is shown for the first; for the second about a third is shown to come from the slots, and the rest is open. Between RWKV's first unit and the attention +8.8 came out instead of -13: 22 of the 26 us that the sum missed in the profiled executions.
- **Term 3** held in kind: the 1.8 us that [rows 7] show at FFN2's end are gone; the sum had put 3.
- **Term 4**: the two starts have 11.3 and 10.0 us more idle time than before; without the waits for weights (term 5) 4.6 in each, put at 4. The size was right, the mechanism in part: 1.2 us of each start are a wait for ScalarE's plain copy (L675), a reader of the kind that was named, and 3.0 are waits for GpSimd's low part of hn (L676), which was not.
- **Term 5** was right in mechanism and a little small: 6.7 and 5.4 us, put at 6 and 4, and e6 takes them away. While GpSimd's operations met VectorE's two-operand ones (2.27 us instead of 1.28), ScalarE's queue waited longer than the 1.3 us of the term gave.
- **Term 6**: 0.82 us a pair, 8.1 in all, put at 6.5.
- **Term 7**: 4.4 and 3.6 us, put at 10 and 2; 1.95 of the 3.6 lie in FFN2's last pair. The wait of FFN1 is the one named, for a cast of wk; its length was less than half of what was put.
- **Term 8**: 2.7 and 2.2 us at the two starts, 1.2 and 1.6 at the two ways down (busy time in each 10 us times the clock missing there), 7.7 together, put at 4.
- **Term 9**: the 5 us for all else in the pairs did not come: FFN2's 270 us of pairs have 0.01 us idle.
- **Rivals (a), (b), (c)**: none in the pairs; of (a), only the late sums of term 5 came. The trace shows operations of both engines longer beside one another (L686 2.27 us instead of 1.28, L104 1.98 instead of 1.22); in the pairs the slack that the prediction gave GpSimd was enough (e11), and where there was none, at the FFN starts, it cost. The Trainium skill, SBUF — State Buffer, section SBUF: two separate sides, has VectorE operations with two SBUF inputs and GpSimd operations that read SBUF lock a shared port against each other; the trace agrees.

Terms 4 to 8 come to 45 us, put at 40.5; the sums of the two FFN stages miss by 6 us more that no window here names.
